# Up projection: the low parts of every second weight piece subtracted on GpSimd instead of VectorE

## The chip, the cores and the metric

The kernel runs on one core of one Trainium2 chip. The core has a matrix engine (TensorE, PE in the profile), a vector engine (VectorE, DVE), a scalar engine (ScalarE, ACT), a general engine (GpSimd, POOL) and an engine that here only issues DMAs (SyncE, SP). Each works through its own queue in order, and semaphores tie them together. The metric is the time of one execution in microseconds on the device; the kernel before took 1499.38 us (median of two runs, 1497.72 and 1501.03).

## What is computed

One transformer block on 256 tokens of width 2048: three attention branches, gates, an output projection, and a feed-forward part. The change lies in the first product of the feed-forward part, the up projection `h2 @ w_up` with 2048 rows and 2 x 5632 columns:

```
h2 = rms_norm(x, g_ffn[l])
u = causal_depthwise_conv(h2 @ w_up[l], conv_w[l], conv_b[l])
u_gate, u_val = jnp.split(u, 2, axis=-1)
x = x + (jax.nn.silu(u_gate) * u_val) @ w_down[l]
```

Inputs and outputs are fp32. The kernel multiplies in a shorter format (fp32r) and keeps the precision by splitting: a weight is its rounded high part `hi` plus the low part `lo = raw - hi`, and so is the activation. The products hi x hi, hi x lo and lo x hi are summed in PSUM.

## The kernel before

The program runs in stages: memory keys and values, input projections with the attention heads beside them, gates and branch products, output projection, up projection, down projection. All weights come in pieces of 128 x 1024 fp32 (512 KB). `piece` (L130) makes each ready: SP issues the DMA into a `raw` tile (L135), ACT casts it into `hi` (L136), DVE subtracts `hi` from `raw` into `lo` (L137). There are four buffers each of `raw`, `hi` and `lo`. So the cast of a piece waits until PE has used up the `hi` of the piece four back, and the DMA of a piece waits until the subtraction of the piece four back has read its `raw`.

The up projection (L729 on) has 22 groups: 11 blocks of four column tiles (`f0` = 0, 4, ... 40), each first for the gate half (`s` = 0) and then for the value half (`s` = 1). A group is eight pieces over the 2048 rows (`k` = 0, 2, ... 14; called piece 0 to 7 below). A piece gives PE 8 pairs of matmuls: 512 columns with `hi` (L739; both parts of the activation stand side by side) and 256 columns with `lo` (L740). The four results of a group stand in four PSUM banks; the next group uses the other four.

While a group is multiplied, the results of the group before are taken out by `conv` (L705), four times: ACT copies one half out of PSUM (L710), DVE adds the other half, which is still in PSUM (L712), DVE multiplies by the row norm (L713), ACT makes the first tap (L716), DVE adds two more (L717, L718). For a gate group ACT adds a SiLU (L720). For a value group DVE multiplies gate and value (L724), ACT rounds the product into its high part (L169) and DVE subtracts the low part (L170). L712 reads one operand from PSUM and one from SBUF; L713, L717, L718, L724, L170 and L137 read two tensors from SBUF.

Except for the first pieces of the program, which are pinned, a scheduler with its own cost estimates sets the order of each engine's queue when the program is built. GpSimd has 46 small instructions in the whole program before, the last at 382 us, and none in the up projection.

Of the kernel before, what the change touches and what calls it, by code (L numbers as in the profile page):

```python
# [9 lines left out]
F32 = mybir.dt.float32  # L10
F32R = mybir.dt.float32r
AF = mybir.ActivationFunctionType
ALU = mybir.AluOpType
# [28 lines left out]
def hybrid_block(  # L42
# [25 lines left out]
    nc = tc.nc  # L68
# [12 lines left out]
    def bank(name):  # L81
        return pp.tile([P, 512], F32, tag="bank", name=name)
# [14 lines left out]
    def later(gen):  # L97
        waiting.append(gen)

    def tick():  # L100
        while waiting and len(active) < WINDOW:
            active.append([waiting.popleft(), 0])
        for a in list(active):
            if a[1] > 0:
                a[1] -= 1
                continue
            try:
                a[1] = next(a[0]) or 0
            except StopIteration:
                active.remove(a)  # L110
# [13 lines left out]
    def pin(ins):  # L124

        if pinned[0]:
            tc.keep_in_program_order(ins)


    def piece(src, a, n, name):  # L130
        raw = wp.tile([P, PIECE], F32, tag="raw", name=f"raw_{name}")
        hi = wp.tile([P, PIECE], F32R, tag="hi", bufs=SBUFS, name=f"hi_{name}")
        lo = wp.tile([P, PIECE], F32R, tag="lo", bufs=SBUFS, name=f"lo_{name}")
        m = a * n
        nc.sync.dma_start(raw[:, :m].rearrange("p (a n) -> p a n", a=a), src)  # L135
        pin(nc.scalar.copy(hi[:, :m], raw[:, :m]))  # L136
        pin(nc.vector.tensor_tensor(lo[:, :m], raw[:, :m], hi[:, :m].bitcast(F32), ALU.subtract))  # L137
        return (
            hi[:, :m].rearrange("p (a n) -> p a n", a=a),
            lo[:, :m].rearrange("p (a n) -> p a n", a=a),  # L140
        )
# [9 lines left out]
    def product(x_of, w, nk, n0, n, name):  # L151

        ps = [bank(f"{name}_{t}") for t in range(NT)]
        wv = w.rearrange("(k p) n -> p k n", p=P)
        for k in range(0, nk, 2):
            a = min(2, nk - k)
            wh, wl = piece(wv[:, k : k + a, n0 : n0 + n], a, n, f"{name}_{k}")
            order = [(j, t) for j in range(a) for t in range(NT)]
            if k + a == nk:
                order.sort(key=lambda jt: jt[1])  # L160
            for j, t in order:
                passes(ps[t][:, :n], x_of(k + j), t, wh[:, j], wl[:, j], k + j == 0, k + j == nk - 1)
            tick()
        return ps
# [212 lines left out]


    wh, wl = piece(kvw[:, :1, :512], 1, 512, "kv0_0")
    transposed(memT, memres, gmem, 0, "mT")  # L380
    keep_busy(2)
    mem_piece(2)
    wh1, wl1 = piece(kvw[:, :1, 512:], 1, 512, "kv0_1")
    kv_part(0, 0, wh[:, 0], wl[:, 0])
    transposed(memT, memres, gmem, 2, "mT")
# [308 lines left out]
    upv = w_up[0].rearrange("(k p) n -> p k n", p=P)  # L694
# [10 lines left out]
    def conv(ps, f, s):  # L705
        if not pads:
            padded()
        ct = s * FT + f
        cr = cp.tile([P, S], F32, tag="cr", bufs=2, name=f"cr_{f}_{s}")
        nc.scalar.copy(cr, ps[:, S:])  # L710
        u = pads[f % 2]
        nc.vector.tensor_tensor(cr, cr, ps[:, :S], ALU.add)  # L712
        nc.vector.tensor_tensor(u[:, 2:], cr, rbc, ALU.mult)  # L713
        y = cp.tile([P, S], F32, tag="y", bufs=6, name=f"y_{f}_{s}")
        tap = lambda j: taps[:, j, ct : ct + 1]
        nc.scalar.activation(y, u[:, 2:], AF.Identity, scale=tap(2), bias=tap(3))  # L716
        nc.vector.scalar_tensor_tensor(y, u[:, 1 : S + 1], tap(1), y, ALU.mult, ALU.add)  # L717
        nc.vector.scalar_tensor_tensor(y, u[:, 0:S], tap(0), y, ALU.mult, ALU.add)  # L718
        if s == 0:
            nc.scalar.activation(y, y, AF.Silu)  # L720
            ys[f] = y
        else:
            g = ys.pop(f)
            nc.vector.tensor_tensor(g, g, y, ALU.mult)  # L724
            split_to(aT[:, f, :], g)
        return
        yield

    for f0 in range(0, FT, 4):  # L729
        for s in range(2):  # L730
            ps = [bank(f"u{f0 + i}_{s}") for i in range(4)]
            c0 = s * D_FF + f0 * P
            for k in range(0, KT, 2):
                hi, lo = piece(upv[:, k : k + 2, c0 : c0 + 512], 2, 512, f"u{f0}_{s}_{k}")
                for j in range(2):
                    first, last = k + j == 0, k + j == KT - 1
                    for i in range(4):
                        c = slice(i * P, (i + 1) * P)
                        nc.tensor.matmul(ps[i], lhsT=hi[:, j, c], rhs=hT[:, k + j, :], start=first, stop=False)  # L739
                        nc.tensor.matmul(  # L740
                            ps[i][:, :S], lhsT=lo[:, j, c], rhs=hT[:, k + j, :S], start=False, stop=last
                        )
                tick()
            for i in range(4):
                later(conv(ps[i], f0 + i, s))
# [121 lines left out]
    for nb, plan in enumerate(plans):  # L867
# [3 lines left out]
        ns, s, e = plan.count("s"), 0, plan.count("s")  # L871
# [54 lines left out]
```

## Time and profile before

| what | us |
|---|---|
| median of the two runs | 1499.38 |
| the two runs | 1497.72, 1501.03 |
| span of the profiled execution, first to last instruction | 1494.4 |
| up projection on PE, first to last matmul start | 766.0 to 1255.2 |
| busy PE in the whole span | 1483.2 |

The profile is of one execution whose own time is known as its span; the median of the runs lies 5.0 us above that span. The page of the profile lists busy time by engine and the costliest groups of instructions; a timeline lists instructions with start, duration, engine, source line, output and inputs. "x2" in a timeline row means two instructions in a row under one entry, whose duration is that of both. What an engine waited for stands in square brackets. The granted clock of TensorE was 1.000 over the whole span.

### The profile page before, as it was taken

How to read it: one execution, taken by the hardware profiler on the slowest of the kernel's cores; microseconds unless marked ns; L12 is line 12 of the kernel's file. 1: busy time of each engine (PE TensorE's matmuls, PEld its weight loads, DVE VectorE, ACT ScalarE, POOL GpSimd, SP SyncE). 2: the span in 40 equal slices, each digit the busy share in tenths (PEclk: the TensorE clock that was granted, in tenths of full speed). 3: DMA queues.
4: the chain of work that ended last, by engine and by line, in shares of the span. 5: the costliest groups of instructions: out<-in, count | busy, mean ns of one | idle time of the engine just before them, and what ended most of it. 6: DMA issues, size and time to landing. Idle time of an engine off the chain costs nothing.

```text
span 1494.4 us, 19871 instructions
## 1 busy us (share of the span) xinstructions
PE 1483.2 (99%) x7429; PEld 1255.9 (84%) x7429; DVE 1014.0 (68%) x1465; ACT 794.0 (53%) x1108; POOL 16.1 (1%) x46
## 2 busy tenths in 40 slices
PE   8999999999999999999999999999999999999998
PEld 6888888888888888888888888888888888888777
DVE  5767566555655646555557778777778778987885
ACT  6755454358544444444456556556556656553552
POOL 0000000001000000000000000000000000000000
PEclk9999999999999999999999999999999999999999
DMA  8665475365666666655555665655656565556554
GB/s 291 193 211 158 126 220 167 119 211 164 188 194 210 185 210 203 185 190 190 184 182 183 198 191 184 196 190 184 198 187 191 186 196 183 199 188 228 185 202 140
DMA packets 138543, 283.62 MB, mean 190 GB/s; under 512 B 9275, under 2 KB 18127, under 8 KB 138447
## 3 DMA queue, kind: packets, MB, share of 16 engines
q1 hardware_dynamic: 137118, 280.26, 59.0%
q10 hardware_dynamic: 1328, 2.11, 0.4%
q8 instruction: 58, 0.95, 0.2%
q14 instruction: 39, 0.31, 0.1%
HBM read 280.23 MB, written 2.10 MB: 189 GB/s over the span
## 4 chain that ended last, share of the span: by engine, by line
PE 95%; DMA 2%; ACT 1%; DVE 1%; issue 0%; POOL 0%; SPq 0%; DVEq 0%; POOLq 0%; ACTq 0%
PE u L739 21%; PE u L740 11%; PE g L147 5%; PE g L148 5%; PE g L149 5%; PE x L797 4%; PE x L798 4%; PE x L799 4%; PE s L147 2%; PE s L149 2%; PE f L147 2%; PE f L149 2%; PE s L148 2%; PE f L148 2%; PE o L147 2%; PE o L149 2%
## 5 line engine op out<-in xcount | busy, mean ns | idle before, releaser
L739 PE MATMUL u<-hT,hi_u 128*128 128x512 f32 x1408 | 488.5, 392 | 0.0
L740 PE MATMUL u<-hT,lo_u 128*128 128x256 f32 x1408 | 395.1, 281 | 0.0
L739 PEld LDWEIGHTS u<-hT,hi_u 128*128 128x128 f32 x1408 | 263.3, 187 | 57.3
L137 DVE TENSOR_TENSOR lo_u<-raw_u,hi_u 128x1024 fp32r<-128x1024 f32 x176 | 215.4, 1224 | 116.0 <-ACT hi_u L136 115.9
L740 PEld LDWEIGHTS u<-hT,lo_u 128*128 128x128 f32 x1408 | 266.8, 189 | 0.0
L136 ACT CAST hi_u<-raw_u 128x1024 fp32r<-128x1024 f32 x176 | 184.7, 1050 | 138.4 <-PE u L739 106.5
L137 DVE TENSOR_TENSOR lo_g<-raw_g,hi_g 128x1024 fp32r<-128x1024 f32 x96 | 117.7, 1229 | 101.3 <-ACT hi_g L136 98.8
L136 ACT CAST hi_g<-raw_g 128x1024 fp32r<-128x1024 f32 x96 | 100.7, 1051 | 121.8 <-PE g L148 97.4
L147 PE MATMUL g<-hi_g,xT 128*128 128x512 f32 x384 | 151.1, 393 | 0.0
L149 PE MATMUL g<-lo_g,xT 128*128 128x512 f32 x384 | 149.8, 390 | 0.0
L148 PE MATMUL g<-hi_g,xT 128*128 128x512 f32 x384 | 149.7, 390 | 0.0
L792 ACT CAST hi_d<-raw_d 128x1024 fp32r<-128x1024 f32 (+1 forms) x88 | 86.7, 993 | 74.6 <-PE x L798 38.7
L793 DVE TENSOR_TENSOR lo_d<-raw_d,hi_d 128x1024 fp32r<-128x1024 f32 (+1 forms) x88 | 99.8, 1148 | 16.2 <-ACT hi_d L792 16.2
L797 PE MATMUL x<-hi_d,aT 128*128 128x512 f32 x268 | 104.4, 390 | 0.0
L799 PE MATMUL x<-lo_d,aT 128*128 128x512 f32 x268 | 104.4, 390 | 0.0
L798 PE MATMUL x<-hi_d,aT 128*128 128x512 f32 x268 | 104.4, 390 | 0.0
L149 PEld LDWEIGHTS g<-lo_g,xT 128*128 128x128 f32 x384 | 72.1, 188 | 15.2
L148 PEld LDWEIGHTS g<-hi_g,xT 128*128 128x128 f32 x384 | 72.2, 188 | 14.5
L147 PEld LDWEIGHTS g<-hi_g,xT 128*128 128x128 f32 x384 | 72.2, 188 | 14.6
L137 DVE TENSOR_TENSOR lo_s<-raw_s,hi_s 128x1024 fp32r<-128x1024 f32 (+1 forms) x40 | 44.7, 1118 | 37.2 <-ACT hi_s L136 37.2
L137 DVE TENSOR_TENSOR lo_f<-raw_f,hi_f 128x1024 fp32r<-128x1024 f32 (+1 forms) x40 | 44.7, 1120 | 34.5 <-ACT hi_f L136 33.0
L136 ACT CAST hi_f<-raw_f 128x1024 fp32r<-128x1024 f32 (+1 forms) x40 | 38.5, 966 | 52.5 <-PE f L148 47.6
(318 smaller groups left out, 2554.3 us busy)
## 6 DMA issues: line engine op xcount, KB each, us to landing
raw_u<-in_w_up_dram SPq DMA_DIRECT2D x176, 512.0 KB, 4.0
raw_g<-in_w_in_dram SPq DMA_DIRECT2D x96, 512.0 KB, 3.6
raw_d<-in_w_down_dram SPq DMA_DIRECT2D x88, 512.0 KB, 4.7
raw_f<-in_w_in_dram SPq DMA_DIRECT2D x32, 512.0 KB, 3.5
raw_s<-in_w_in_dram SPq DMA_DIRECT2D x32, 512.0 KB, 3.4
raw_o<-in_w_out_dram SPq DMA_DIRECT2D x32, 512.0 KB, 4.7
raw_kv<-in_w_mem_kv_dram SPq DMA_DIRECT2D x15, 512.0 KB, 5.4
raw_b<-in_w_br_fox_dram SPq DMA_DIRECT2D x12, 512.0 KB, 4.0
```

Of the source, the lines that this page charges most:

```text
L136: pin(nc.scalar.copy(hi[:, :m], raw[:, :m]))
L137: pin(nc.vector.tensor_tensor(lo[:, :m], raw[:, :m], hi[:, :m].bitcast(F32), ALU.subtract))
L147: nc.tensor.matmul(o, lhsT=xh, rhs=wh, start=first, stop=False)
L148: nc.tensor.matmul(o, lhsT=xl, rhs=wh, start=False, stop=False)
L149: nc.tensor.matmul(o, lhsT=xh, rhs=wl, start=False, stop=last)
L739: nc.tensor.matmul(ps[i], lhsT=hi[:, j, c], rhs=hT[:, k + j, :], start=first, stop=False)
L740: nc.tensor.matmul(ps[i][:, :S], lhsT=lo[:, j, c], rhs=hT[:, k + j, :S], start=False, stop=last)
L792: nc.scalar.copy(hi[:, :n], src)
L793: nc.vector.tensor_tensor(lo[:, :n], src, hi[:, :n].bitcast(F32), ALU.subtract)
L797: nc.tensor.matmul(o, lhsT=ah, rhs=w[0], start=first, stop=False)
L798: nc.tensor.matmul(o, lhsT=al, rhs=w[0], start=False, stop=False)
L799: nc.tensor.matmul(o, lhsT=ah, rhs=w[1], start=False, stop=last)
```

## The change

In the up projection, pieces 1, 3, 5 and 7 of each group (`k // 2` mod 4 equal to 1 or 3) have their L137 subtraction issued on GpSimd; pieces 0, 2, 4 and 6 stay on VectorE. That is 88 of 176 subtractions. No other call of `piece` passes the new argument.

```diff
-    def piece(src, a, n, name):
+    def piece(src, a, n, name, low=None):
...
-        pin(nc.vector.tensor_tensor(lo[:, :m], raw[:, :m], hi[:, :m].bitcast(F32), ALU.subtract))
+        pin((low or nc.vector).tensor_tensor(lo[:, :m], raw[:, :m], hi[:, :m].bitcast(F32), ALU.subtract))
...
-                hi, lo = piece(upv[:, k : k + 2, c0 : c0 + 512], 2, 512, f"u{f0}_{s}_{k}")
+                low = nc.gpsimd if (k // 2) % 4 in (1, 3) else None
+                hi, lo = piece(upv[:, k : k + 2, c0 : c0 + 512], 2, 512, f"u{f0}_{s}_{k}", low)
```

GpSimd's queue in this stage then holds these 88 subtractions and nothing else, in the order of the pieces. With four buffers and every second piece on GpSimd, a buffer of `raw`, `hi` or `lo` always belongs to the same engine. The scheduler also orders the rest anew. Two places in the group `f0` = 20, `s` = 0 show it; `lo_u20_0_8` is the low part of its piece 4 (`k` = 8), `lo_u20_0_10` that of piece 5, and `cr_18`, `y_18`, `y_19`, `u_0`, `u_1` are tiles of the `conv` of the group before. Lines up to 733 keep their numbers in the changed kernel; the matmuls of L739 and L740 become L740 and L741.

On VectorE, around the low part of piece 4, before:

```order
L712 TENSOR_TENSOR cr_18_1_8481<-cr_18_1_8481,u18_1_8197 128x256
L170 TENSOR_TENSOR aT_6209<-y_16_0_8225,aT_6209 128x256
L170 TENSOR_TENSOR aT_6209<-y_17_0_8234,aT_6209 128x256
L713 TENSOR_TENSOR u_0_6457<-cr_18_1_8481,rbc_5524 128x256
L712 TENSOR_TENSOR cr_19_1_8492<-cr_19_1_8492,u19_1_8198 128x256
L137 TENSOR_TENSOR lo_u20_0_8_8549<-raw_u20_0_8_8547,hi_u20_0_8_8548 128x1024
L717 SCALAR_TENSOR_TENSOR y_18_1_8485<-u_0_6457,taps_108,y_18_1_8485 128x256
L713 TENSOR_TENSOR u_1_6459<-cr_19_1_8492,rbc_5524 128x256
L718 SCALAR_TENSOR_TENSOR y_18_1_8485<-u_0_6457,taps_108,y_18_1_8485 128x256
L137 TENSOR_TENSOR lo_u20_0_10_8571<-raw_u20_0_10_8569,hi_u20_0_10_8570 128x1024
```

and now:

```order
L712 TENSOR_TENSOR cr_18_1_8481<-cr_18_1_8481,u18_1_8197 128x256
L724 TENSOR_TENSOR y_17_0_8234<-y_17_0_8234,y_17_1_8452 128x256
L170 TENSOR_TENSOR aT_6209<-y_16_0_8225,aT_6209 128x256
L713 TENSOR_TENSOR u_0_6457<-cr_18_1_8481,rbc_5524 128x256
L170 TENSOR_TENSOR aT_6209<-y_17_0_8234,aT_6209 128x256
L712 TENSOR_TENSOR cr_19_1_8492<-cr_19_1_8492,u19_1_8198 128x256
L717 SCALAR_TENSOR_TENSOR y_18_1_8485<-u_0_6457,taps_108,y_18_1_8485 128x256
L713 TENSOR_TENSOR u_1_6459<-cr_19_1_8492,rbc_5524 128x256
L718 SCALAR_TENSOR_TENSOR y_18_1_8485<-u_0_6457,taps_108,y_18_1_8485 128x256
L137 TENSOR_TENSOR lo_u20_0_8_8549<-raw_u20_0_8_8547,hi_u20_0_8_8548 128x1024
```

Piece 5's subtraction has left VectorE, and piece 4's now stands behind three more steps of `conv` (L717, L713, L718).

On ScalarE, from the cast of piece 4 to the cast of piece 6, before:

```order
L136 CAST hi_u20_0_8_8548<-raw_u20_0_8_8547 128x1024
L169 CAST aT_6209<-y_16_0_8225 128x256
L169 CAST aT_6209<-y_17_0_8234 128x256
L136 CAST hi_u20_0_10_8570<-raw_u20_0_10_8569 128x1024
L716 ACTIVATE y_18_1_8485<-u_0_6457,taps_108 128x256
L716 ACTIVATE y_19_1_8496<-u_1_6459,taps_108 128x256
L136 CAST hi_u20_0_12_8592<-raw_u20_0_12_8591 128x1024
```

and now:

```order
L136 CAST hi_u20_0_8_8548<-raw_u20_0_8_8547 128x1024
L169 CAST aT_6209<-y_16_0_8225 128x256
L169 CAST aT_6209<-y_17_0_8234 128x256
L716 ACTIVATE y_18_1_8485<-u_0_6457,taps_108 128x256
L136 CAST hi_u20_0_10_8570<-raw_u20_0_10_8569 128x1024
L716 ACTIVATE y_19_1_8496<-u_1_6459,taps_108 128x256
L136 CAST hi_u20_0_12_8592<-raw_u20_0_12_8591 128x1024
```

The cast of piece 5, on which GpSimd's subtraction of that piece waits, has moved behind one L716, and so behind the L713 that feeds it.

## Prediction

> **What bounds the kernel now.** I read the page's busy times first, then the up projection by itself with the view of windows, then the timeline of one group. The page and the window over the steady part of the stage:
>
> ```profile
> span 1494.4 us, 19871 instructions
> ...
> PE 1483.2 (99%) x7429; PEld 1255.9 (84%) x7429; DVE 1014.0 (68%) x1465; ACT 794.0 (53%) x1108; POOL 16.1 (1%) x46
> ...
> 788.00:1255.00 467.00, 467.00 (x2697) 412.18 (x2696) 353.42 (x586) 275.70 (x423) 0.00 (x0) 1.00 0.60 190
> ```
>
> PE is busy for all 467 us of the window at full clock, DVE for 353 (76%), ACT for 276 (59%), GpSimd not at all. PE is idle for only 1494.4 - 1483.2 = 11.2 us in the whole span. So there is next to nothing to win: DVE is relieved, but nobody waits for DVE long enough to show on PE. The question is whether the low parts still arrive before PE needs them.
>
> For that I take one group apart (`f0` = 20, `s` = 0), chosen because it carries a value group's `conv`, the heavier sort. PE's pace comes first, then DVE's rows (start, duration, what) and ACT's:
>
> ```profile
> 988.05 0.39 PE L739 MATMUL u<-hT,hi_u 128*128 128x512 f32 x1
> 988.40 0.39 PE L739 MATMUL u<-hT,hi_u 128*128 128x512 f32 x1
> ...
> 999.03 0.28 PE L740 MATMUL u<-hT,lo_u 128*128 128x256 f32 x1
> 999.14 0.39 PE L739 MATMUL u<-hT,hi_u 128*128 128x512 f32 x1
> ```
>
> ```profile
> 988.66 0.77 DVE L712 TENSOR_TENSOR cr<-cr,u 128x256 f32<-128x256 f32 x2
> 989.34 0.75 DVE L713 TENSOR_TENSOR u<-cr,rbc 128x256 f32<-128x256 f32 x2
> 990.26 1.23 DVE L137 TENSOR_TENSOR lo_u<-raw_u,hi_u 128x1024 fp32r<-128x1024 f32 x1 [0.16 <-ACT hi_u L136]
> 991.40 0.88 DVE L717 SCALAR_TENSOR_TENSOR y<-u,taps,y 128x256 f32<-128x256 f32 x2
> 992.19 0.88 DVE L718 SCALAR_TENSOR_TENSOR y<-u,taps,y 128x256 f32<-128x256 f32 x2
> 992.99 0.76 DVE L724 TENSOR_TENSOR y<-y,y 128x256 f32<-128x256 f32 x2
> 993.65 0.42 DVE L712 TENSOR_TENSOR cr<-cr,u 128x256 f32<-128x256 f32 x1
> 993.99 0.76 DVE L170 TENSOR_TENSOR aT<-y,aT 128x256 fp32r<-128x256 f32 x2
> 994.66 0.42 DVE L713 TENSOR_TENSOR u<-cr,rbc 128x256 f32<-128x256 f32 x1
> 994.99 0.42 DVE L712 TENSOR_TENSOR cr<-cr,u 128x256 f32<-128x256 f32 x1
> 995.33 1.22 DVE L137 TENSOR_TENSOR lo_u<-raw_u,hi_u 128x1024 fp32r<-128x1024 f32 x1
> ...
> 997.59 1.22 DVE L137 TENSOR_TENSOR lo_u<-raw_u,hi_u 128x1024 fp32r<-128x1024 f32 x1
> ```
>
> ```profile
> 989.17 1.06 ACT L136 CAST hi_u<-raw_u 128x1024 fp32r<-128x1024 f32 x1 [0.20 <-PE u L739]
> 990.13 1.09 ACT L716 ACTIVATE y<-u,taps 128x256 f32<-128x256 f32 x2
> ...
> 991.99 1.05 ACT L136 CAST hi_u<-raw_u 128x1024 fp32r<-128x1024 f32 x1 [0.25 <-ACT cr L710]
> 993.44 0.74 ACT L169 CAST aT<-y 128x256 fp32r<-128x256 f32 x2 [0.40 <-DVE y L724]
> 994.76 1.05 ACT L136 CAST hi_u<-raw_u 128x1024 fp32r<-128x1024 f32 x1 [0.58 <-PE u L739]
> 995.72 0.60 ACT L716 ACTIVATE y<-u,taps 128x256 f32<-128x256 f32 x1
> ```
>
> From 988.05 to 999.14 lie 32 pairs of matmuls, 0.347 us each, so a piece takes 8 x 0.347 = 2.77 us and a group 22.2. ACT's cast at 989.17 waited for the last `hi` matmul of the group before, which is the fourth of the rows at 988.05, 988.40 and so on; the group therefore starts at 988.05 + 3 x 0.347 = 989.09. Piece 4 starts at 989.09 + 4 x 2.77 = 1000.18 and reads its `lo` with its first L740, 0.23 us later (the L740 row stands 0.11 ahead of the next L739): by 1000.41. Its `lo` was done at 995.33 + 1.22 = 996.55, that is 3.86 us early. That is the cover. It is thinnest at piece 4, since DVE runs without a gap from 988.66 on.
>
> **What the subtraction costs on GpSimd.** The trace has no two-input operation on GpSimd. The nearest rows are a fill and a select, which reads one input:
>
> ```profile
> L579 POOL TENSOR_SCALAR_AFFINE_SELECT sb<-sb x24: 292/292/1274, 316.6 to 382.1; 128x128 f32<-128x128 f32 x24
> ...
> L78 POOL MEMSET sm_pad<- 128x160 f32 x1 | 0.2, 231 | 0.3 <-POOLq L912 0.3
> ...
> L223 POOL MEMSET ones<- 128x128 f32 x1 | 0.2, 204 | 0.0
> ```
>
> Two fills give (231 - 204) / 32 = 0.84 ns per element and 204 - 128 x 0.84 = 96 ns fixed. The select's 292 ns less 96, over 128 elements, are 1.53 ns per element with one input. Twice that for two inputs gives 1024 x 3.06 + 96 = 3.2 us: the value I take. Bounds: 2.34 us if two inputs cost no more than the select's whole 292 ns per 128 (and 0.96 us if only the rate of a fill counted, which I leave out, since the select with one input is already slower); 4.7 us if each input costs the select's whole duration. The subtraction on DVE takes 1.22.
>
> By the Trainium skill, GPSIMD Engine Reference, section 3.1 (Elementwise), a two-input fp32 operation on 2048 elements was measured at 4497 ns; half of it would be an estimate of 2.25 us, and the first term below would come out near 9 us. No run here shows it yet.
>
> **Beside DVE.** The two engines are not independent. Two places of the timeline in the stage of the heads, where selects fall on subtractions of DVE:
>
> ```profile
> 317.60 1.52 POOL L579 TENSOR_SCALAR_AFFINE_SELECT sb<-sb 128x128 f32<-128x128 f32 x2 [0.49 <-DVE sb L597]
> 317.61 1.35 DVE L137 TENSOR_TENSOR lo_g<-raw_g,hi_g 128x1024 fp32r<-128x1024 f32 x1
> ```
>
> ```profile
> 349.96 3.67 DVE L137 TENSOR_TENSOR lo_g<-raw_g,hi_g 128x1024 fp32r<-128x1024 f32 x3
> 350.21 2.35 POOL L579 TENSOR_SCALAR_AFFINE_SELECT sb<-sb 128x128 f32<-128x128 f32 x2 [4.08 <-DVE sb L597]
> ```
>
> Two selects alone take 0.58 us. Here they take 1.52 and 2.35: a select that meets a running subtraction ends only with it (the longest is 1274 ns). In the first place the select was ahead by 0.01 us, and it is DVE's subtraction that is longer, 1.35 for 1.22. In the second, three subtractions stand back to back and the two selects still come through, one at each joint. I read this as turns: an operation that reads two tensors from SBUF on DVE and one that reads on GpSimd exclude each other while they run, and who waits goes next. That DVE would stand still for the whole length of a long GpSimd operation is an inference from 0.13 us. The Trainium skill, SBUF — State Buffer, section Who interferes with whom, says just this: whichever is second is blocked until the first has finished. By it the walk below holds; the selects agree.
>
> **The walk through the group.** Let T be the time of the subtraction on GpSimd. DVE's steps back to back come from the rows: 0.34 us for L712, L713, L724, L170 (0.42 less the overlap with the next), 0.40 for L717 and L718, 1.14 for L137.
>
> - Piece 3. Its cast ends at 989.17 + 1.06 = 990.23. DVE then has nothing for the moment: its next step, L717, waits for ACT's L716, done near 990.75. So GpSimd starts at 990.25 and DVE stands still until 990.25 + T.
> - DVE then runs L717, L718, L717, L724, L718, L712, L724, L170, L713: 4 x 0.40 + 5 x 0.34 = 3.3 us.
> - ACT now has one L716 (0.60) ahead of the cast of piece 5 (1.05); the cast ends some 1.65 to 1.7 us after that L713, at 5.0 us on this count. DVE meanwhile does L170, L712, L717 (which waits for the same L716), L713 and L718, the last until 5.27. So GpSimd's request for piece 5 is there 0.3 us before DVE reaches piece 4's subtraction, and GpSimd goes first: 5.27 to 5.27 + T.
> - Piece 4's subtraction runs after it and ends at 990.25 + T + 5.27 + T + 1.23 = 996.75 + 2T.
>
> PE needs it by 1000.41, so PE stalls for 2T - 3.66 us: 1.0 at 2.34, 2.7 at 3.2, 5.7 at 4.7. Ten groups carry a value group's `conv` (the eleventh falls into the down projection): 10 x 2.7 = 27 us. In the eleven groups with a gate's `conv`, L724 and L170 are missing and piece 4 stands behind 7 steps after the first hold, so on the clock of this group its `lo` is done at 990.25 + T + 2.6 + 1.2 = 997.3, well ahead of 1000.41; no stall there from this order.
>
> The second term is the time in which the two exclude each other. With a gate's `conv` a group asks for 4 x 1.14 + 4 x (0.34 + 0.40 + 0.40) = 9.1 us of DVE plus 4 x 3.2 of GpSimd = 21.9, of 22.2. The four L712 read PSUM and need not exclude GpSimd, but they stand in DVE's queue behind what is blocked; with their 1.36 it is 23.3, or 1.1 over. 11 x 1.1 = 12 us, or nothing if they overlap; I take the 12, since nothing puts GpSimd's operation beside them. In a value's group the same count gives 26.0, 3.8 over, of which the stall of 2.7 is already counted; I leave the rest out.
>
> **Other parts.** The 88 subtractions taken off DVE (88 x 1.22 = 107 us) give nothing back, as PE did not wait for them. The DMA of the piece four on waits on SP for the subtraction to read `raw`, and all later issues queue behind it:
>
> ```profile
> raw_u<-in_w_up_dram SPq DMA_DIRECT2D x176, 512.0 KB, 4.0
> ```
>
> Landing 4.0, cast 1.05 and T = 3.2 make 8.3 us of the 11.1 in which four pieces pass; 2.8 us are left for waits, so it costs nothing, up to T near 5. The casts on ACT have 41% of idle time to move in.
>
> **The sum.** Against the profiled execution: 1494.4 + 27 + 12 = 1533; with the 5.0 us by which the median lies above the span, 1499.4 + 39 = 1538, which is 2.6% slower.
>
> **The rivals.**
> - A short subtraction, T near 2.3 (the select's row is the argument; the page of the skill named above speaks for it too): the stall is 1.0 us in ten groups and the second term vanishes, 1499 + 10 = 1509, within 2%.
> - No cost at all, the other side: the place is the joint where piece 5 on GpSimd and piece 4 on DVE meet. If DVE goes first there, piece 4 is done at 996.7 + T, in time up to T = 3.7, and piece 5 too up to 3.3. For it: the margin in the walk is only 0.3 us. Then 1499. Against: the cast of piece 5 hangs on the same L713 as DVE, so both move together.
> - DVE does not yield: it keeps the port while it has work, and GpSimd gets on only in gaps. Then piece 3's `lo`, due at 989.09 + 3 x 2.77 + 0.23 = 997.6, ends after DVE's block. That block starts at 990.75 and lasts the 6.5 us of the walk and four more steps (1.5), to 998.7; GpSimd has had the gap of 0.5 us before it and some 0.4 in it, and 2.3 are left, so to 1001: a stall of 3.3 in ten groups. With a gate's `conv` the block ends near 996.5, and the stall is 1.2 in eleven: 1499 + 46 = 1545. For it: DVE's three subtractions took 3.67, little more than three steps.
> - GpSimd saturates, T near 4.7: a gate's group asks for 9.1 + 1.4 + 18.8 = 29.3 (7.1 over 22.2), a value's for 32.0 (9.8 over): 11 x 7.1 + 10 x 9.8 = 176, so 1675. Only the upper bound of the price speaks for it.
> - A gain: the earlier even pieces would have to meet a PE that waits, and there are 11.2 us of idle PE in all. That the change does not do what it says is ruled out by the order.
>
> **Chances.** Two per cent, or 30 us, is about what a measurement of this kernel can tell from no change. Forecast 0.44, its own range 1520 to 1575 (T from 2.8 to 3.7); of it 0.06 stay within 2%. Short subtraction 0.20, no cost 0.12: both within 2%. DVE does not yield 0.13 and saturation 0.07: slower. Gain 0.04. So slower 0.58, within 0.38, faster 0.04. The range from 1500 to 1590 leaves out saturation, the gain and half of the case without cost, 0.17.
>
> **What would show it.** In the profile after: L137 on POOL 88 times with a mean near 3.2 us (2.3 or 4.7 for the rivals); L717 or L718 on DVE in rows of T or more, where it waited for GpSimd; PE idle before the `lo` matmul (L741 there) in ten groups of 22, at piece 4, put down to DVE's `lo`. If PE waits for POOL's `lo` at piece 3 instead, DVE does not yield. If PE is busy throughout and the time is at 1500, the cover held. A GpSimd subtraction under 2.3 us, or DVE rows that do not grow beside it, would make the forecast wrong.

## The result, and the profile after

The changed kernel takes 1511.08 us (median; 1509.65 to 1512.50), against 1499.38: a ratio of 1.0081, 95% interval 1.0062 to 1.0100. It is slower by about 12 us, a third of the 39 that were forecast. The time lies below the forecast's own range of 1520 to 1575; the wide range of 1500 to 1590 holds it only because it takes in the rival of a short subtraction.

The page of the profile after (its profiled execution has a span of 1507.9 us, 13.5 above that of before), the busy line and the groups that deal with the low parts:

```profile
span 1507.9 us, 19892 instructions
...
PE 1490.0 (99%) x7429; PEld 1256.6 (83%) x7429; DVE 1024.6 (68%) x1377; ACT 792.1 (53%) x1108; POOL 235.0 (16%) x134
...
L741 PE MATMUL u<-hT,lo_u 128*128 128x256 f32 x1408 | 395.7, 281 | 6.7 <-DVE lo_u L137 6.7
L137 POOL TENSOR_TENSOR lo_u<-raw_u,hi_u 128x1024 fp32r<-128x1024 f32 x88 | 218.9, 2487 | 660.5 <-ACT hi_u L136 645.7
```

The same groups before:

```profile
L740 PE MATMUL u<-hT,lo_u 128*128 128x256 f32 x1408 | 395.1, 281 | 0.0
...
L137 DVE TENSOR_TENSOR lo_u<-raw_u,hi_u 128x1024 fp32r<-128x1024 f32 x176 | 215.4, 1224 | 116.0 <-ACT hi_u L136 115.9
```

Two things are new. GpSimd's subtraction appears 88 times at a mean of 2.49 us. And PE's `lo` matmul (L740 before, L741 here) has 6.7 us of idle time in front of it where it had none, put down to DVE's `lo`, not to GpSimd's. VectorE's busy time has gone up, 1014.0 to 1024.6, although 88 subtractions left it: the rows that remain are longer. The answer for the tile `lo_u` gives shortest, median and longest of each engine's subtractions, and who waited:

```profile
L137 DVE TENSOR_TENSOR lo_u<-raw_u,hi_u x88: 1217/1226/3443, 757.2 to 1256.6; 128x1024 fp32r<-128x1024 f32 x88
L137 POOL TENSOR_TENSOR lo_u<-raw_u,hi_u x88: 2393/2410/3030, 760.0 to 1257.6; 128x1024 fp32r<-128x1024 f32 x88
...
  PEld u L741: 9.9, 10
  PE u L741: 6.7, 10
```

PE waits for a `lo` exactly ten times, and its weight loads (PEld) with it. The first and last starts of the `hi` matmuls give the length of the up projection, before and after:

```profile
L739 PE MATMUL u<-hT,hi_u x1408: 389/391/476, 766.0 to 1255.0; 128*128 128x512 f32 x176
```

```profile
L740 PE MATMUL u<-hT,hi_u x1408: 389/391/476, 764.3 to 1265.8; 128*128 128x512 f32 x176
```

489.0 us became 501.5: 12.5 us, of the 13.5 by which the spans of these two profiled executions differ. The same group as in the prediction (`f0` = 20, `s` = 0), in the timelines of GpSimd, DVE and PE:

```profile
992.64 2.42 POOL L137 TENSOR_TENSOR lo_u<-raw_u,hi_u 128x1024 fp32r<-128x1024 f32 x1 [3.15 <-ACT hi_u L136]
999.99 2.50 POOL L137 TENSOR_TENSOR lo_u<-raw_u,hi_u 128x1024 fp32r<-128x1024 f32 x1 [4.93 <-ACT hi_u L136]
```

```profile
993.10 2.24 DVE L717 SCALAR_TENSOR_TENSOR y<-u,taps,y 128x256 f32<-128x256 f32 x1 [0.70 <-ACT y L716]
995.38 0.48 DVE L718 SCALAR_TENSOR_TENSOR y<-u,taps,y 128x256 f32<-128x256 f32 x1
...
999.74 0.48 DVE L718 SCALAR_TENSOR_TENSOR y<-u,taps,y 128x256 f32<-128x256 f32 x1
1000.14 3.43 DVE L137 TENSOR_TENSOR lo_u<-raw_u,hi_u 128x1024 fp32r<-128x1024 f32 x1
```

```profile
1002.48 0.39 PE L740 MATMUL u<-hT,hi_u 128*128 128x512 f32 x1
1003.62 0.39 PE L741 MATMUL u<-hT,lo_u 128*128 128x256 f32 x1 [0.75 <-DVE lo_u L137]
1003.85 0.39 PE L740 MATMUL u<-hT,hi_u 128*128 128x512 f32 x1
```

It reads like the walk. Piece 3 on GpSimd holds VectorE's L717 for 2.24 instead of 0.48 us. Piece 5 on GpSimd starts at 999.99, just ahead of piece 4 on VectorE, whose subtraction then takes 3.43 us. It ends at 1003.57, and PE's first `lo` matmul of piece 4 starts at 1003.62, 1.14 us after its `hi` matmul. Before, the same two matmuls lie 0.23 us apart:

```profile
1000.18 0.39 PE L739 MATMUL u<-hT,hi_u 128*128 128x512 f32 x1
1000.41 0.28 PE L740 MATMUL u<-hT,lo_u 128*128 128x256 f32 x1
```

### The profile page after: what moved, and what is told of

Same layout as the page of the kernel before. It is cut to its first block, busy times and chain, and to the rows that moved or that the text cites. A ratio compares the mean times of both kernels' runs of the same rounds, so it can differ in the third digit from the quotient of the medians.

```text
span 1507.9 us, 19892 instructions
## 1 busy us (share of the span) xinstructions
PE 1490.0 (99%) x7429; PEld 1256.6 (83%) x7429; DVE 1024.6 (68%) x1377; ACT 792.1 (53%) x1108; POOL 235.0 (16%) x134
## 4 chain that ended last, share of the span: by engine, by line
PE 89%; DVE 7%; ACT 1%; issue 1%; DMA 1%; POOL 0%; SPq 0%; DVEq 0%; POOLq 0%
PE u L740 17%; PE u L741 9%; PE g L147 5%; PE g L149 5%; PE g L148 5%; PE x L800 4%; PE x L798 4%; PE x L799 4%; DVE lo_u L137 2%; PE s L147 2%; PE s L149 2%; PE f L147 2%; PE f L148 2%; PE s L148 2%; PE f L149 2%; DVE y L717 2%
## 5 line engine op out<-in xcount | busy, mean ns | idle before, releaser
L740 PE MATMUL u<-hT,hi_u 128*128 128x512 f32 x1408 | 492.2, 394 | 0.0
L741 PE MATMUL u<-hT,lo_u 128*128 128x256 f32 x1408 | 395.7, 281 | 6.7 <-DVE lo_u L137 6.7
L137 POOL TENSOR_TENSOR lo_u<-raw_u,hi_u 128x1024 fp32r<-128x1024 f32 x88 | 218.9, 2487 | 660.5 <-ACT hi_u L136 645.7
L740 PEld LDWEIGHTS u<-hT,hi_u 128*128 128x128 f32 x1408 | 263.8, 187 | 60.2
L741 PEld LDWEIGHTS u<-hT,lo_u 128*128 128x128 f32 x1408 | 266.0, 189 | 9.9 <-DVE lo_u L137 9.9
L137 DVE TENSOR_TENSOR lo_u<-raw_u,hi_u 128x1024 fp32r<-128x1024 f32 x88 | 156.9, 1783 | 102.8 <-ACT hi_u L136 102.8
L137 DVE TENSOR_TENSOR lo_g<-raw_g,hi_g 128x1024 fp32r<-128x1024 f32 x96 | 117.7, 1228 | 101.4 <-ACT hi_g L136 98.9
L717 DVE SCALAR_TENSOR_TENSOR y<-u,taps,y 128x256 f32<-128x256 f32 x88 | 78.8, 896 | 14.9 <-ACT y L716 14.9
L137 DVE TENSOR_TENSOR lo_s<-raw_s,hi_s 128x1024 fp32r<-128x1024 f32 (+1 forms) x40 | 44.7, 1118 | 37.2 <-ACT hi_s L136 37.2
```

Of the source, the lines that this page charges most:

```text
L137: pin((low or nc.vector).tensor_tensor(lo[:, :m], raw[:, :m], hi[:, :m].bitcast(F32), ALU.subtract))
L741: nc.tensor.matmul(ps[i][:, :S], lhsT=lo[:, j, c], rhs=hT[:, k + j, :S], start=False, stop=last)
```

## The experiments

All ratios are to the kernel before, run on the same chip, with 95% intervals. "Up" is the length of the up projection as above.

| run | on GpSimd | ratio | interval | up, us |
|---|---|---|---|---|
| the change | pieces 1, 3, 5, 7 | 1.0081 | 1.0062 to 1.0100 | 501.5 |
| e1_p35 | 3, 5 | 1.0084 | 1.0069 to 1.0099 | 502.9 |
| e2_p17 | 1, 7 | 0.9997 | 0.9988 to 1.0006 | 489.0 |
| e3_p3 | 3 | 1.0002 | 0.9992 to 1.0011 | 489.0 |
| e4_p5 | 5 | 1.0004 | 0.9994 to 1.0014 | 489.0 |
| e7_spread | 1, 3, 5, 7, later conv | 0.9994 | 0.9985 to 1.0004 | 489.0 |
| e8_spread_dve | none, later conv | 1.0003 | 0.9993 to 1.0012 | 489.0 |
| e10_late | none, piece 4 late | 1.0123 | 1.0106 to 1.0140 | 508.7 |
| e11_p13457 | 1, 3, 4, 5, 7 | 1.0046 | 1.0031 to 1.0061 | 497.2 |

**Which pieces.** The theory was the joint of the walk, the place where piece 5 on GpSimd meets piece 4 on VectorE: the cost takes piece 3 and piece 5 together. The rivals were that the time in which VectorE stands still for GpSimd ("port time" below) costs wherever it falls, or that the new order alone costs.

```diff
-                low = nc.gpsimd if (k // 2) % 4 in (1, 3) else None
+                low = nc.gpsimd if k // 2 in (3, 5) else None
```

(and `(1, 7)`, `(3,)`, `(5,)`).

> Only pieces 3 and 5 of each group on GpSimd (44 subtractions instead of 88). Theory of the joint (piece 3 holds VectorE for T, then piece 5 goes ahead of piece 4's subtraction for another T; stall 2T - 3.66 = 1.2 us with T = 2.41 as measured, in ten groups): the same time as with all 88, some 12 us above the kernel before, ratio 1.007 to 1.009, ten waits of PE for VectorE's lo. Rival, the port time lost counts wherever it falls: half of it, +6 us, 1.004.

> Only pieces 1 and 7 on GpSimd (44 subtractions); the scheduler's order around piece 4 is that of the kernel before. Theory of the joint: no stall, ratio 0.999 to 1.001. Rival, port time counts wherever it falls: +6 us, 1.004.

> Only piece 3 on GpSimd (22 subtractions). VectorE's order up to piece 4 is that of the changed kernel: piece 4 stands behind three more steps of conv, and GpSimd's piece 3 holds VectorE once. Theory of the joint: piece 4's lo ends at 996.7 + T = 999.1 on the clock of the profiled group, 1.3 us before PE needs it, so no stall, ratio 0.999 to 1.001. Rival, the new order by itself is the cause: +12 us, 1.008.

> Only piece 5 on GpSimd (22 subtractions). Its cast stands ahead of L716 again and piece 4 is not held by piece 3. Theory of the joint: piece 4's subtraction is under way when GpSimd asks, so no stall, ratio 0.999 to 1.001. Rival, piece 5 on GpSimd is enough: +12 us, 1.008.

Half of the subtractions cost as much as all of them if they are pieces 3 and 5, and nothing if they are 1 and 7. Either piece alone costs nothing. So neither rival holds. That pieces 3 and 5 cost the same to a microsecond or two as all 88 is in part chance: PE's stalls at piece 4 make about 8 of the 14 us there, and 9.4 of 12.5 in the change; the rest is the change of pace in the last section. The run with piece 3 alone has VectorE's order of the changed kernel up to piece 4, so that order by itself is not the cause. Its timelines of GpSimd and DVE in the same group:

```profile
989.13 2.41 POOL L137 TENSOR_TENSOR lo_u<-raw_u,hi_u 128x1024 fp32r<-128x1024 f32 x1 [19.78 <-ACT hi_u L136]
```

```profile
989.59 2.23 DVE L717 SCALAR_TENSOR_TENSOR y<-u,taps,y 128x256 f32<-128x256 f32 x1 [0.67 <-ACT y L716]
...
996.21 0.48 DVE L718 SCALAR_TENSOR_TENSOR y<-u,taps,y 128x256 f32<-128x256 f32 x1
996.61 1.22 DVE L137 TENSOR_TENSOR lo_u<-raw_u,hi_u 128x1024 fp32r<-128x1024 f32 x1
```

The first hold is there (L717 at 2.23), the second is not (piece 4 at 1.22, done at 997.83). So piece 5 on GpSimd, the second hold, is needed. The run with piece 5 alone has the order of before around piece 4; piece 5 alone in the order of the changed kernel was not tried, so that the first hold is needed too is argued from the walk and not shown by itself.

**All 88, without the joint.** The `conv` of the third and fourth tile starts two pieces later, which puts piece 4's subtraction ahead of most of their steps in VectorE's queue.

```diff
     def conv(ps, f, s):
+        if f % 4 >= 2 and f < FT - 4:
+            yield 2
```

> All 88 subtractions on GpSimd as in the changed kernel, but the conv of the third and fourth tile of a group starts two pieces later, so that piece 4's subtraction on VectorE stands ahead of the second pair's steps. Theory of the joint: piece 4's lo ends near 996.9 on the clock of the profiled group, before GpSimd's piece 5 asks; no stall, ratio 0.999 to 1.001 to the kernel before, with all of GpSimd's port time still there. Rival, port time counts wherever it falls: the 12 us stay, 1.008.

> Control: the same later start of conv in the kernel before, all subtractions on VectorE. All theories: ratio 0.999 to 1.001.

In the first of them VectorE loses nearly the same time to GpSimd (its page has VectorE busy for 1022.3 us, against 1024.6 in the change, and GpSimd for 241.7 against 235.0) and the 12 us are gone. In the same group piece 4's subtraction is now done, at 996.23, when GpSimd's piece 5 starts:

```profile
995.01 1.22 DVE L137 TENSOR_TENSOR lo_u<-raw_u,hi_u 128x1024 fp32r<-128x1024 f32 x1
```

```profile
996.23 2.94 POOL L137 TENSOR_TENSOR lo_u<-raw_u,hi_u 128x1024 fp32r<-128x1024 f32 x1 [4.07 <-ACT hi_u L136]
```

The control does not move. So the cost lies in the joint and not in the work moved.

**The price and the exclusion by themselves.** A kernel of phases: each phase copies its inputs afresh, then issues rows of one operation on GpSimd (`p_` tiles) and of one on VectorE (`d_` tiles). What follows is from the profile of one execution.

```
phase("palone", None, "sub")                       # GpSimd alone; also 512, 256 columns, copy
phase("both",  "sub", "sub", nd=6, npl=5)          # both, 1024 columns
phase("small", "sub", "sub", nd=16, npl=4, wd=256) # VectorE with 256 columns
phase("psum",  "psum", "sub", nd=10, npl=4)        # one VectorE operand in PSUM
phase("red",   "red",  "sub", nd=6, npl=4)         # VectorE reduces one tensor
phase("fill",  "sub", "fill", nd=6, npl=6)         # GpSimd only writes
```

> A kernel of phases that computes nothing of the reference: subtractions on GpSimd and VectorE alone and beside each other. GpSimd alone: 2.4 us at 1024 columns as in the profile after; if the price goes per element, near 1.25 at 512 and 0.7 at 256. A copy (one input) on GpSimd tells whether two inputs cost twice one: about half of 2.4 if so, 1.6 if it goes at the select's 1.53 ns per element. Beside VectorE's subtractions of 1024: by turns, VectorE's rows near 1.2 + 2.4 = 3.6 and GpSimd's near 3.6; if VectorE does not yield, its rows stay at 1.22 and GpSimd's grow by all of VectorE's work; if they share, both grow by a part. With one VectorE operand in PSUM, a VectorE reduction of one tensor, a GpSimd fill, or ScalarE copies beside it: no growth on either side.

The groups of its profile by form (mean ns of one behind the comma), alone first:

```profile
L101 POOL TENSOR_TENSOR p_palone<-X_palone,Y_palone 128x1024 fp32r<-128x1024 f32 x4 | 9.4, 2338 | 0.3
...
L101 POOL TENSOR_TENSOR p_p<-X_p,Y_p 128x512 fp32r<-128x512 f32 x4 | 5.0, 1261 | 0.3
L103 POOL CAST p_pcopy<-X_pcopy 128x1024 fp32r<-128x1024 f32 x4 | 4.2, 1039 | 0.3
...
L101 POOL TENSOR_TENSOR p_p<-X_p,Y_p 128x256 fp32r<-128x256 f32 x4 | 2.9, 722 | 0.3
```

and the answers for the tiles of the mixed phases (shortest, median, longest):

```profile
L101 POOL TENSOR_TENSOR p_both<-X_both,Y_both x5: 3198/3200/3202, 79.3 to 92.4; 128x1024 fp32r<-128x1024 f32 x5
```

```profile
L94 DVE TENSOR_TENSOR d_both<-X_both,Y_both x6: 3244/3244/3245, 77.0 to 93.4; 128x1024 fp32r<-128x1024 f32 x6
```

```profile
L94 DVE TENSOR_TENSOR d_small<-X_small,Y_small x16: 424/426/2446, 100.0 to 117.0; 128x256 fp32r<-128x256 f32 x16
```

```profile
L96 DVE TENSOR_TENSOR d_psum<-X_psum,bank x10: 686/686/689, 120.9 to 127.4; 128x512 fp32r<-128x512 f32 x10
```

```profile
L98 DVE TENSOR_REDUCE d_red<-X_red x6: 1220/1220/1220, 135.1 to 141.3; 128x1 f32<-128x1024 f32 x6
```

Two inputs cost (2338 - 1261) / 512 = 2.10 ns per element and 184 ns fixed; a copy of 1024 costs 1039 ns in all, not the 1.6 us at the select's 1.53 ns per element. In the mixed phase both engines go by turns: every row of either is near 3.2 us, not the 3.6 expected. VectorE loses 3.244 - 1.226 = 2.02 us per turn, less than GpSimd's 2.34, so about 0.3 us of the two overlaps. A small VectorE operation loses the same 2.02 (2446 instead of 426 ns), once for each GpSimd operation. With one operand in PSUM, a single input on VectorE, GpSimd only filling (its rows 951 ns, VectorE's median 1226) or ScalarE copying (GpSimd's mean 2341), neither grows. That agrees with the Trainium skill, SBUF — State Buffer, section Who interferes with whom, which names a VectorE instruction with two SBUF inputs against a GpSimd instruction that reads SBUF as a case that contends. The lock that it calls exclusive is a little looser in these rows, by the 0.3 us.

**Lateness without GpSimd.** VectorE repeats piece 4's subtraction three times in the ten groups:

```diff
-        pin(nc.vector.tensor_tensor(lo[:, :m], raw[:, :m], hi[:, :m].bitcast(F32), ALU.subtract))
+        for _ in range(times):
+            pin(nc.vector.tensor_tensor(lo[:, :m], raw[:, :m], hi[:, :m].bitcast(F32), ALU.subtract))
...
+                times = 4 if k == 8 and s == 0 and f0 > 0 else 1
```

> No GpSimd at all: the kernel before, in which VectorE repeats piece 4's subtraction three times in the ten groups that carry a value group's conv, so that its lo comes late by a delay on VectorE alone. By the rows of the kernel before, its last subtraction ends near 1002.6 on the clock of the profiled group, 2.2 us after PE needs it. If lateness of this one tile is the whole cost: ten waits of PE of about 2.2 us, +22 us (1.015). If PE's pace after a stall (353 instead of 347 ns a pair in parts of the up projection after the change) comes from stalls and not from GpSimd, it shows here too and adds up to 9 us; if it comes from GpSimd, the pace stays at 347.

The ratio of 1.0123 is some 18 us, a little less than the 22 expected. The up projection is 19.7 us longer, and ten waits of the weight loads for VectorE's `lo` are put down, 16.5 us together. PE runs four `hi` matmuls of piece 4 here before the first `lo`, so a part of the delay is filled:

```profile
1005.99 1.09 PE L741 MATMUL u<-hT,hi_u 128*128 128x512 f32 x4
1008.41 0.74 PE L742 MATMUL u<-hT,lo_u 128*128 128x256 f32 x4 [1.33 <-DVE lo_u L138]
1008.99 0.40 PE L741 MATMUL u<-hT,hi_u 128*128 128x512 f32 x1
```

The four pairs take 3.00 us instead of 4 x 0.347 = 1.39. Ten such delays make about 15 us. So a delay of piece 4 on VectorE alone costs in the same way. The pace of PE also changes here without any GpSimd in the stage; that is taken up below.

**More on GpSimd, piece 4 too.**

```diff
-                low = nc.gpsimd if (k // 2) % 4 in (1, 3) else None
+                low = nc.gpsimd if k // 2 in (1, 3, 4, 5, 7) else None
```

> Pieces 1, 3, 4, 5 and 7 on GpSimd: 110 subtractions instead of 88, so more work on the slower engine, but piece 4 no longer stands in VectorE's queue behind conv. Theory of the joint: GpSimd does pieces 3 and 4 by 995.5 on the clock of the profiled group, five us before PE needs piece 4, and piece 5 by about 1002.4, 0.8 us ahead; no stall, ratio 0.999 to 1.002. Rival, port time counts wherever it falls: 110/88 of the 12 us, +15 us, 1.010.

Neither came: 1.0046, between the theory's 1.000 and the rival's 1.010. The page of this run puts down a single wait for a `lo` of this stage, of a weight load for GpSimd's, where the theory had none:

```profile
L741 PEld LDWEIGHTS u<-hT,lo_u 128*128 128x128 f32 x1408 | 266.0, 189 | 0.5 <-POOL lo_u L137 0.5
```

It lies in a group with a gate's `conv`, where GpSimd's subtraction of piece 5 ran until 846.73:

```profile
844.29 2.44 POOL L137 TENSOR_TENSOR lo_u<-raw_u,hi_u 128x1024 fp32r<-128x1024 f32 x1 [1.94 <-ACT hi_u L136]
```

```profile
846.25 0.39 PE L740 MATMUL u<-hT,hi_u 128*128 128x512 f32 x1
846.78 0.39 PE L741 MATMUL u<-hT,lo_u 128*128 128x256 f32 x1
```

0.53 instead of 0.23 us: 0.3 us lost. The other 8 us of its up projection come from what PE does afterwards, and that was not in any of the theories.

None of these kernels is faster than the one before, and with 11.2 us of idle PE in its whole span there was little to find. A fifth buffer of `hi` and `lo`, which would widen the cover by one piece, was not tried.

## Why the prediction came out as it did

**What bounds the kernel: right.** PE was busy throughout, the 107 us taken off VectorE gave nothing back, and the cover of 3.86 us at piece 4 was the place that mattered: all ten waits are there (pieces 20, 36, 52 and so on to 164 of the stage, counted from 0), in the ten groups with a value's `conv`, and none in a gate's.

**The walk: right in its order.** GpSimd's piece 5 went first in all ten groups, by 0.15 us between the starts of the two rows and 0.23 us before VectorE's L718 ended; the prediction counted 0.3. The first hold, the second hold and the late piece 4 are in the rows. Without the second hold the cost was gone in the same order (piece 3 alone); without the first it was gone too, but there the order had changed as well (piece 5 alone).

**The price of the subtraction on GpSimd: wrong, and this is the step that failed.** The prediction took 96 ns of a fill as the fixed part of a select, so that the select's input cost 1.53 ns per element, and then "Twice that for two inputs gives 1024 x 3.06 + 96 = 3.2 us". Measured alone it is 2.34 us: 184 ns fixed and 2.10 ns per element. If the select has the 184 ns of the subtraction, its 292 leave 0.84 ns per element, the rate of a fill; the copy of 1024 leaves (1039 - 184) / 1024 = 0.83. So the fixed part was taken from an operation that does not read, and what it left too much per element was scaled to eight times the elements and doubled. The lower bound, 2.34, was the right number, for a reason that the prediction did not have. The estimate from the Trainium skill, GPSIMD Engine Reference, section 3.1, 2.25 us, was within 4%. By the walk it gives 10 x 0.84 = 8.4 us, where the prediction wrote near 9.

With 2.41 us, the median in the kernel, the walk's 2T - 3.66 gives 1.16 us for each group. Measured were gaps of 1.13 us (seven times) and 0.91 (three times) where 0.23 is normal, and 0.11 more on the next matmul: 1.0 or 0.8 us. The walk is a little long because it let VectorE stand still for the whole T and then run the next step in full: in the rows above L717 ends 0.28 us and piece 4's subtraction 1.08 us after GpSimd's, where they last 0.48 and 1.22 by themselves. The three shorter gaps follow stretches of the slower pace described below, in which PE reaches piece 4 later by 32 x 6.5 ns = 0.2 us. Ten groups make 7 x 1.01 + 3 x 0.79 = 9.4 us.

**The second term: wrong with the first.** The 12 us for a port that is asked for longer than the group lasts rested on T = 3.2. With 2.41 a gate's group asks for 9.1 + 9.6 + 1.4 = 20.1 of 22.2 us and the term is nothing; the spread kernel, with all 88 and a ratio of 0.9994, shows it.

**What was left out** is the change of pace below. In the profiled execution of the change it makes the remaining 3 us: 9.4 + 3.1 = 12.5. The prediction also took 2% for about what a measurement of this kernel can tell; the interval from 1.0062 to 1.0100 tells 0.8% from nothing.

**The rivals.** "A short subtraction" was the case that came, at a chance of 0.20: 1509 was its time and 1511 was measured. That the two are so near is in part luck: its ten us are the 9.4 of the stalls, and the 3 of the pace were in no count. "Saturation" falls by the price, 2.41 us in the kernel and not 4.7. "No cost" fell at its own place: VectorE did not go first at the joint. "DVE does not yield" falls by the turns, and PE waits for no `lo` of GpSimd in the change. The DMAs and the casts cost nothing, as written: with 88 on GpSimd and `conv` spread the stage lasts 489.0.

## What to carry to other kernels

Work moved off a busy engine onto a slower one is not paid by its total but at the tightest deadline of the loop: find the tile that arrives with the least lead, and ask what the moved work puts in front of it. Two engines that exclude each other count as one queue there, and two holds in a row can break a cover that each of them leaves whole. An operation's price should be scaled from rows that do the same kind of access, with the fixed part taken from two sizes of one operation; where no such rows exist, the forecast should lean on the bound that has a measured operation behind it.

## What the runs showed of the hardware that was not expected

After a gap PE can go on at a different pace. In the fast one, 32 pairs of matmuls (512 and 256 columns) take 11.09 us, 346.6 ns a pair; in the other 11.30 us, 353.1 ns, 1.9% longer. The first and the 33rd `hi` matmul of two stretches of the changed kernel:

```profile
979.95 0.39 PE L740 MATMUL u<-hT,hi_u 128*128 128x512 f32 x1
...
991.04 0.39 PE L740 MATMUL u<-hT,hi_u 128*128 128x512 f32 x1
```

```profile
1009.85 0.40 PE L740 MATMUL u<-hT,hi_u 128*128 128x512 f32 x1
...
1021.15 0.40 PE L740 MATMUL u<-hT,hi_u 128*128 128x512 f32 x1
```

In the ten traces of the whole kernel, the pace changed only at a gap, and stayed until another gap: in the change it is slow from the stall at 1003 to that at 1095 and from 1186 to the end, 170 us in all, which costs 170 x (1 - 346.6 / 353.1) = 3.1 us. The six kernels without a late `lo`, the one before among them, hold 489.0 us to a tenth. The kernel with piece 4 late and no GpSimd in the stage shows both paces too, so GpSimd is not needed for it. In the run with five pieces on GpSimd a single gap of 0.3 us at 846.8 was followed by the slow pace to the end of the stage:

```profile
999.64 0.40 PE L740 MATMUL u<-hT,hi_u 128*128 128x512 f32 x1
...
1010.94 0.40 PE L740 MATMUL u<-hT,hi_u 128*128 128x512 f32 x1
```

and the view of windows over that part (the granted clock stands behind the engines):

```profile
850.00:1255.00 405.00, 405.00 (x2294) 351.17 (x2294) 335.07 (x415) 232.08 (x360) 233.24 (x91) 1.00 0.60 186
```

415 us at that pace cost 415 x (1 - 346.6 / 353.1) = 415 x 0.0184 = 7.6 us, nearly all that its up projection lost (8.2). The granted clock is 1.00 in that window, so it is not the clock as the profile reports it. What sets the pace, and why a gap sometimes changes it and sometimes not, stays open.
